# In a bidirectional gated recurrence, the convolution's centre tap is moved ahead of the square roots on ScalarE and its lower part ahead of the scans on VectorE

## The chip, the cores and the metric

The kernel runs on one core of one Trainium2 chip. The metric is the time of one execution in microseconds (us) on the device, as the median of several runs. Engines are named as the profile names them: PE is TensorE's matmul and PEld its weight load, DVE is VectorE, ACT is ScalarE, POOL is GpSimd, SP is SyncE; a q behind a name is the engine's queue.

## The reference, cut to what matters

The whole kernel computes one layer of a diffusion backbone: latent attention and a bidirectional recurrence (RG-LRU) side by side, a gated merge, and a convolutional feed-forward part. The change lies in the recurrence. For each of its 1280 channels it takes the projected input `xb`, runs a centred convolution of width 4 over time, forms two gates per direction from the result, and scans over time, forwards and backwards:

```python
xc = dwconv(xb, lru_conv_w, lru_conv_b, 2, 1)        # four taps, shifts -2, -1, 0, +1
r = sigmoid(xc_blocks @ w_a + b_a)                    # 10 blocks of 128 channels, 2 directions
i = sigmoid(xc_blocks @ w_x + b_x)
log_a = -8 * r * softplus(-lam)
a = exp(log_a)
u = sqrt(-expm1(2 * log_a)) * (i * xc)
h[t] = a[t] * h[t - 1] + u[t]                         # hb: the same from the end
y_b = ((hf + hb) * gelu(yb)) @ w_o_lru
```

Time has 256 context steps and 1024 latent steps, 1280 columns together.

## The kernel before

Products are made in fp32 from two parts: a higher part `hi` (a copy rounded to fp32r, made by ScalarE) and a lower part `lo` (the source minus `hi`, made by VectorE). Each product is three matmuls: hi by hi, hi by lo, lo by hi (`product`, `split`).

The recurrence is `lru`. It works through ten blocks of 128 channels (`for b in range(NB + 1)`; the eleventh round only finishes the last block). TensorE, ScalarE and VectorE run in the order in which the code is written (`manual_schedule`); for GpSimd and SyncE a scheduler sets the order. The recurrence is a pipeline of two blocks: in round `b`, the projections and gates of block `b` are made, and the two scans (`chains`, one for each direction) of block `b - 1`.

What TensorE does in a round: `z(3)` projects `xb` of the block over three column segments into the PSUM tile `z`; `z(2)` projects the gelu branch over two; a merge gate is projected into two tiles `f`; then `gate` is called four times and multiplies the convolution's parts `xh` and `xl` with the gate weights into tiles `g`. `z` and `g` share one PSUM tag with two buffers, so the third `g` needs the buffer from which the first sigmoid (`gate`, L692) reads.

What ScalarE does in a round: a copy `whi` and a copy `ghi` (weights' higher parts), two exponentials (`exp`, L706), two square roots (`root`, L716), the convolution's centre tap with its bias (`xc`, L677), the higher part `xh` (L684), a weight copy, the gelu `gy` (L779), two sigmoids of the merge gate (`gst`, L1218), a weight copy, four gate sigmoids (L692), and two tanh (L703). An ACT_TABLE_LOAD stands where the next function needs another table.

What VectorE does in a round: for each direction three steps between the exponential and the root (`less`, L711, L712, L713); six steps for the other three taps of the convolution (L680 to L682, over the latent and the context columns), which read the product in PSUM and add onto `xc`; for each direction a multiply by the root (L720) and the scans (L723 and L724 forwards, L726 backwards); the lower part `xl` (L771); the gating of the output, weights' lower parts, and three or four steps of the late modulation. These last multiply a weight tile `mw` by a scalar and add onto `macc` (L1238, L1240). GpSimd fetches the `mw` tiles (two buffers), and after every eighth it sums `macc` over the partitions and adds a bias row (L1243, L1246). GpSimd also stores the merge gates (`gld`, from a stage with two buffers) and the recurrence's output (`lrud`).

Of the kernel before, what the change touches and what calls it, by code (L numbers as in the profile page):

```python
# [12 lines left out]
F32 = mybir.dt.float32  # L13
F32R = mybir.dt.float32r
AF = mybir.ActivationFunctionType
OP = mybir.AluOpType
# [7 lines left out]
A = T + C  # L24
# [83 lines left out]
class Block:  # L108
# [494 lines left out]
    def lru(self):  # L603
        tc, nc, a = self.tc, self.nc, self.a
# [27 lines left out]
        with self.pool("lru") as sp, tc.manual_schedule(engines={mybir.EngineType.PE, mybir.EngineType.Activation,  # L632
# [22 lines left out]
            def prepare():  # L655
                if raws:
                    ready.append(self._load_w(None, D, raws.pop(0)))
                    fetch()
# [5 lines left out]
            def z(nseg):  # L664
                ps = pp.tile([P, 3 * 512], F32, tag="z", bufs=2, name=self.name("z"))
                times([(ps[:, c0:c0 + n], self.hrhs(g)) for g, (c0, n) in enumerate(SEGS[:nseg])])
                return ps

            def merge_gate(m):
                st = self.merge_gate(m, *ready.pop(0))  # L670
                prepare()
                nc.gpsimd.dma_start(self.gl_d[m], st)

            def conv(b, ps):
                xc = T5("xc", "xc")
                cw = lambda k: self.vec("cw", 4 * b + k)
                nc.scalar.activation(xc, ps[:, :A], AF.Identity, bias=self.vec("cb", b), scale=cw(2))  # L677
                for c0, n in ((0, T), (T, C)):
                    s, d = ps[:, c0:c0 + n], xc[:, c0:c0 + n]
                    nc.vector.scalar_tensor_tensor(d[:, 2:], s[:, :n - 2], cw(0), d[:, 2:], op0=OP.mult, op1=OP.add)  # L680
                    nc.vector.scalar_tensor_tensor(d[:, 1:], s[:, :n - 1], cw(1), d[:, 1:], op0=OP.mult, op1=OP.add)
                    nc.vector.scalar_tensor_tensor(d[:, :n - 1], s[:, 1:], cw(3), d[:, :n - 1], op0=OP.mult, op1=OP.add)  # L682
                xh, xl = T5("xh", "xh", F32R), T5("xl", "xl", F32R)
                nc.scalar.activation(xh, xc, AF.Copy)  # L684
                return xc, xh, xl

            def gate(b, d, x, w, xh, xl):
                pg = pp.tile([P, 3 * 512], F32, tag="z", bufs=2, name=self.name("g"))
                outs = [(pg[:, c0:c0 + n], lambda k, p, c0=c0, n=n: (xh if p == 0 else xl)[:, c0:c0 + n]) for c0, n in SEGS]
                self.product(outs, lambda k, p: w[p][:, 2 * d + x, :], 1)  # L690
                t = T5(("ta", "tb")[x], "gate", bufs=2)
                nc.scalar.activation(t, pg[:, :A], AF.Sigmoid, bias=self.vec(("ba", "bx")[x], 2 * b + d))  # L692
                return t

            class Chain:
# [19 lines left out]
                def root(c):  # L715
                    nc.scalar.activation(c.s, c.s, AF.Sqrt, scale=-1.0)  # L716

                def scan(c):
                    av, u, s = c.r, c.u, c.s
                    nc.vector.tensor_tensor(u, u, s, op=OP.mult)  # L720
                    cs, ls = slice(T, A), slice(0, T)
                    if c.d == 0:
                        nc.vector.tensor_tensor_scan(s[:, cs], av[:, cs], u[:, cs], 0.0, op0=OP.mult, op1=OP.add)  # L723
                        nc.vector.tensor_tensor_scan(s[:, ls], av[:, ls], u[:, ls], s[:, A - 1:A], op0=OP.mult, op1=OP.add)  # L724
                    else:
                        nc.vector.tensor_tensor_scan(s[:, ::-1], av[:, ::-1], u[:, ::-1], 0.0, op0=OP.mult, op1=OP.add)  # L726

            def gated(gy, hf, hb):
                nc.vector.tensor_tensor(hf[:, :T], hf[:, :T], hb[:, :T], op=OP.add)
                nc.vector.tensor_tensor(gy, gy, hf[:, :T], op=OP.mult)  # L730

            def out(b, gy):
                so = sp.tile([P, 2, T], F32R, tag="lo", bufs=1, name=self.name("lruo"))
                self.split(gy, so[:, 0, :], so[:, 1, :])
                nc.gpsimd.dma_start(self.lru_d[b], so.bitcast(F32))

            def gate_weights(b):
                w = [sp.tile([P, 4, P], F32R, tag=t, bufs=1, name=self.name(t)) for t in ("ghi", "glo")]
                self.split(raws.pop(0)[:, :4 * P], *[t.rearrange("p a b -> p (a b)") for t in w])
                fetch()  # L740
                return w
# [5 lines left out]
            gy, chains = None, []  # L747
            for b in range(NB + 1):
                new = b < NB

                rest = iter(fills[b - 1][1:] if not new else ())
                if new:
                    ps = z(3)
                    prepare()
                    w = gate_weights(b)
                for c in chains:
                    c.exp()
                for c in chains:
                    c.less()
                    if new:  # L760
                        c.root()
                if not new:
                    merge_gate(next(rest))
                    for c in chains:
                        c.root()
                if new:
                    xc, xh, xl = conv(b, ps)
                for c in chains[:1]:
                    c.scan()
                if new:  # L770
                    nc.vector.tensor_tensor(xl, xc, xh.bitcast(F32), op=OP.subtract)  # L771
                for c in chains[1:]:
                    c.scan()
                old = gy
                if new:
                    ps = z(2)
                    prepare()
                    gy = sp.tile([P, T], F32, tag="gy", bufs=2, name=self.name("gy"))
                    nc.scalar.activation(gy, ps[:, :T], AF.Gelu_apprx_tanh)  # L779
                for m in islice(rest, 1):  # L780
                    merge_gate(m)
                if chains:
                    gated(old, chains[0].s, chains[1].s)
                if not new:
                    out(b - 1, old)
                for _ in range(3):
                    next(late, None)
                for m in rest if not new else fills[b][:1]:
                    merge_gate(m)
                if not new:  # L790
                    break
                t = [gate(b, d, x, w, xh, xl) for d in range(2) for x in range(2)]
                if chains:
                    out(b - 1, old)
                chains = [Chain(b, d, t[2 * d], t[2 * d + 1]) for d in range(2)]
                for c in chains:
                    nc.vector.tensor_tensor(c.u, c.u, xc, op=OP.mult)
                    c.tanh()
                next(late, None)
# [1337 lines left out]
```

## Time and profile before

| | |
|---|---|
| median of 3 runs | 1879.92 us (1878.91 to 1880.41) |
| the profiled execution's own time | 1877.24 us |
| its span in the profile | 1875.5 us |
| PE busy | 1829.7 us, 98% |
| PEld busy | 1466.0 us, 78% |
| DVE busy | 1390.0 us, 74% |
| ACT busy | 970.3 us, 52% |
| POOL busy | 383.1 us, 20% |
| mean granted clock of TensorE | 0.994 of full speed |

The span is what the profile sees of one execution; the execution's own time has a little more around it. Busy shares are means over the whole span. The recurrence lies between about 225 and 705 us; times in the trace count from the span's start. A granted clock of 1 is the higher of TensorE's two levels, 2.4 GHz, and one of 0.5 the lower, 1.2 GHz. In a row of the timeline, the text in brackets is how long the engine was idle before the row, and what ended that.

### The profile page before, as it was taken

What the parts mean: (1) busy time and instruction counts of PE and PEld (TensorE: products, weight loads), DVE (VectorE), ACT (ScalarE), POOL (GpSimd) and SP (SyncE); (2) the same over time, 40 slices, a digit from 0 to 9 for tenths busy, and PEclk for the clock granted to TensorE, in tenths of its full rate; (3) what the DMA queues carried; (4) which work ended last, traced back from release to release, by engine and by line L of the source; (5) the groups of instructions that cost most, each with busy time, mean ns of one, the idle gap of its engine ahead of it and who ended that gap; (6) DMA issues with size and microseconds to landing.
All of it is one profiled execution on the core that took longest, in us unless ns stands there. A gap on an engine that the chain in (4) does not pass through costs nothing.

```text
span 1875.5 us, 22292 instructions
## 1 busy us (share of the span) xinstructions
PE 1829.7 (98%) x8180; PEld 1466.0 (78%) x8180; DVE 1390.0 (74%) x1691; ACT 970.3 (52%) x1319; POOL 383.1 (20%) x360
## 2 busy tenths in 40 slices
PE   8999999999999999999999999998999999999998
PEld 3788878887777877888887778876888888888886
DVE  6544668888888858787877775688877777776565
ACT  6434355656565656676666623364444444445452
POOL 0011402020202004676667400000101000010000
PEclk9999999999999999999999999999999999999999
DMA  8125532323332249343432483123443444398671
GB/s 342 57 98 193 216 121 107 129 107 129 118 118 96 95 146 308 109 125 101 125 100 93 135 304 153 64 82 102 185 152 143 155 174 152 140 356 293 214 246 63
DMA packets 109267, 288.29 MB, mean 154 GB/s; under 512 B 14353, under 2 KB 26403, under 8 KB 106854
## 3 DMA queue, kind: packets, MB, share of 16 engines
q1 hardware_dynamic: 85094, 196.04, 30.7%
q0 software_dynamic: 23632, 89.26, 12.4%
q10 hardware_dynamic: 432, 1.57, 0.3%
q8 instruction: 64, 1.05, 0.2%
q14 instruction: 45, 0.37, 0.1%
HBM read 203.30 MB, written 83.52 MB: 153 GB/s over the span
## 4 chain that ended last, share of the span: by engine, by line
PE 61%; issue 24%; DVE 6%; POOL 3%; DMA 3%; ACT 2%; SPq 0%; DVEq 0%; POOLq 0%; ACTq 0%
PE u L1546 18%; PE da L1930 6%; PE f L1038 6%; PE db L1930 4%; PE o L920 4%; PE z L161 2%; PE s L896 2%; PE s L895 2%; PE s L894 2%; PE yo L161 2%; DMA mw<-in_wmod_dram 2%; PE kvps L378 2%; PE x L867 2%; PE f L161 2%; PE ya L161 1%
## 5 line engine op out<-in xcount | busy, mean ns | idle before, releaser
L1546 PE MATMUL u<-b,op 128*128 128x512 f32 x1320 | 312.8, 396 | 7.0 <-ACT pg L1554 2.8
L1546 PEld LDWEIGHTS u<-b,op 128*128 128x128 f32 x1320 | 247.1, 188 | 69.1 <-ACT pg L1554 3.7
L161 PE MATMUL z<-hx,whi 128*128 128x512 f32 x736 | 211.8, 397 | 0.0
L914 POOL TENSOR_TENSOR acc<-acc,p 128x512 f32<-128x512 f32 x120 | 175.8, 1465 | 60.4 <-ACT p L900 56.9
L906 DVE TENSOR_TENSOR pl<-p,ph 128x512 fp32r<-128x512 f32 x160 | 159.9, 1002 | 28.5 <-ACT ph L902 28.1
L161 PE MATMUL f<-hx,whi 128*128 128x512 f32 x480 | 151.0, 396 | 0.0
L900 ACT ACTIVATE p<-s 128x512 f32<-128x512 f32 x160 | 95.6, 597 | 100.0 <-PE s L896 67.7
L161 PEld LDWEIGHTS z<-hx,whi 128*128 128x128 f32 x736 | 126.8, 189 | 25.6
L1915 DVE TENSOR_TENSOR dp<-dr,dp 128x1024 fp32r<-128x1024 f32 x77 | 93.2, 1223 | 56.4 <-PE da L1930 29.9
L1546 PE MATMUL u<-h,op 128*128 128x512 f32 x528 | 127.6, 394 | 0.0
L1546 PEld LDWEIGHTS u<-h,op 128*128 128x128 f32 x528 | 98.4, 188 | 22.8
L161 PE MATMUL z<-hx,wlo 128*128 128x512 f32 x368 | 116.1, 397 | 0.0
L123 DVE TENSOR_TENSOR wlo<-wraw,whi 128x1024 fp32r<-128x1024 f32 (+2 forms) x60 | 67.4, 1125 | 64.1 <-ACT whi L122 64.0
L1038 PE MATMUL f<-l,whi 128*128 128x512 f32 x320 | 108.9, 396 | 0.0
L1930 PE MATMUL da<-dp,dp 128*128 128x512 f32 x352 | 108.4, 389 | 0.0
L161 PEld LDWEIGHTS f<-hx,whi 128*128 128x128 f32 x480 | 90.0, 188 | 21.8 <-ACT r L448 0.2
L1910 ACT ACTIVATE dp<-dr 128x1024 fp32r<-128x1024 f32 x77 | 79.2, 1056 | 52.6 <-PE da L1930 24.8
L868 DVE TENSOR_REDUCE pm<-x 128x1 f32<-128x512 f32 x128 | 83.6, 684 | 29.7 <-PE x L867 20.3
L902 ACT ACTIVATE ph<-p 128x512 fp32r<-128x512 f32 x160 | 101.2, 632 | 5.1
L1512 ACT ACTIVATE op<-wraw 128x512 fp32r<-128x512 f32 x90 | 54.0, 624 | 85.2 <-DVE wraw L1503 62.2
L161 PE MATMUL f<-hx,wlo 128*128 128x512 f32 x240 | 94.9, 395 | 0.0
L1516 DVE TENSOR_TENSOR op<-wraw,op 128x512 fp32r<-128x512 f32 x90 | 61.5, 688 | 33.6 <-ACT op L1512 33.6
(367 smaller groups left out, 3994.4 us busy)
## 6 DMA issues: line engine op xcount, KB each, us to landing
wraw<-in_wz_dram SPq DMA_DIRECT2D x41, 512.0 KB
dr<-da SPq DMA_DIRECT2D x79, 256.0 KB
da<-pg POOLq DMA_DIRECT2D x33, 512.0 KB, 3.7
mw<-in_wmod_dram POOLq DMA_DIRECT2D x32, 512.0 KB, 3.8
wraw<-in_wup_dram SPq DMA_DIRECT2D x23, 512.0 KB
wdr<-in_wdn_dram SPq DMA_DIRECT2D x22, 512.0 KB
db<-wdr POOLq DMA_DIRECT2D x22, 512.0 KB, 2.9
dr<-db SPq DMA_DIRECT2D x44, 256.0 KB
```

The costliest lines, as they stand in the source:

```text
L161: nc.tensor.matmul(ps, wts(k, wp), rhs(k, rp), start=(k == 0 and j == 0), stop=(k == nk - 1 and j == 2))
L868: nc.vector.tensor_reduce(r.pm[:, t, c:c + 1], ps, axis=mybir.AxisListType.X, op=OP.max)
L900: nc.scalar.activation(r.p[b], r.s.pop(b), AF.Exp, scale=SCALE)
L902: nc.scalar.activation(r.ph[b], r.p[b], AF.Copy)
L906: nc.vector.tensor_tensor(r.pl[b], r.p[b], r.ph[b].bitcast(F32), op=OP.subtract)
L914: by.tensor_tensor(r.acc, r.p[0] if b == 1 else r.acc, r.p[b], op=OP.add)
L920: nc.tensor.matmul(r.o, r.v[b // 2][:, b % 2, :], pt.pop(b), start=(b == 0 and n == 0), stop=(b == NT - 1 and n == 1))
L1038: nc.tensor.matmul(f, (hi, lo)[wp][:, k * P:(k + 1) * P], lt[5 * j + k][rp][:, g * 512:(g + 1) * 512], start=(j == 0 and q == 0), stop=(j ...
L1546: self.nc.tensor.matmul(ps, w[wp][:, k * P:(k + 1) * P], self.right(i, k, rp), start=(first and k == 0 and j == 0), stop=(final and k == 3 ...
L1910: self.nc.scalar.activation(self.parts[n][0], self.raws[n], AF.Copy)
L1915: self.nc.vector.tensor_tensor(lo, self.raws.pop(n), hi.bitcast(F32), op=OP.subtract)
L1930: self.nc.tensor.matmul(ps, parts[lp][:, t * P:(t + 1) * P], parts[rp][:, 512:], start=(first and k == 0 and j == 0), stop=(final and k == ...
```

## The change

The function `conv` made the centre tap, the three other taps and the higher part. The centre tap is now a function of its own, `centre`, which is called right after the exponentials. The first multiply of the scan is a step of its own, `drive`. The lower part `xl` stands behind the first chain's `drive` and ahead of its scans.

```diff
-            def conv(b, ps):
+            def centre(b, ps):
                 xc = T5("xc", "xc")
+                nc.scalar.activation(xc, ps[:, :A], AF.Identity, bias=self.vec("cb", b), scale=self.vec("cw", 4 * b + 2))
+                return xc
+
+            def conv(b, ps, xc):
                 cw = lambda k: self.vec("cw", 4 * b + k)
-                nc.scalar.activation(xc, ps[:, :A], AF.Identity, bias=self.vec("cb", b), scale=cw(2))
...
-                return xc, xh, xl
+                return xh, xl
...
+                def drive(c):
+                    nc.vector.tensor_tensor(c.u, c.u, c.s, op=OP.mult)
+
                 def scan(c):
                     av, u, s = c.r, c.u, c.s
-                    nc.vector.tensor_tensor(u, u, s, op=OP.mult)
...
                 for c in chains:
                     c.exp()
+                if new:
+                    xc = centre(b, ps)
                 for c in chains:
                     c.less()
...
                 if new:
-                    xc, xh, xl = conv(b, ps)
+                    xh, xl = conv(b, ps, xc)
+                for c in chains[:1]:
+                    c.drive()
+                if new:
+                    nc.vector.tensor_tensor(xl, xc, xh.bitcast(F32), op=OP.subtract)
                 for c in chains[:1]:
                     c.scan()
-                if new:
-                    nc.vector.tensor_tensor(xl, xc, xh.bitcast(F32), op=OP.subtract)
                 for c in chains[1:]:
+                    c.drive()
                     c.scan()
```

On ScalarE, in the round that makes block 4, the exponentials (`gate`), the table load and the two roots (`s`) stood ahead of the centre tap `xc`. Before:

```order
L706 ACTIVATE gate_2879<-gate_2879,sp_1748 128x1280
L706 ACTIVATE gate_2903<-gate_2903,sp_1748 128x1280
L716 ACT_TABLE_LOAD
L716 ACTIVATE s_2921<-s_2921 128x1280
L716 ACTIVATE s_2922<-s_2922 128x1280
L677 ACTIVATE xc_3025<-z_2930,vecs 128x1280
L684 ACTIVATE xh_3033<-xc_3025 128x1280
```

And of the change, at the same place:

```order
L709 ACTIVATE gate_2879<-gate_2879,sp_1748 128x1280
L709 ACTIVATE gate_2903<-gate_2903,sp_1748 128x1280
L676 ACTIVATE xc_3017<-z_2930,vecs 128x1280
L719 ACT_TABLE_LOAD
L719 ACTIVATE s_2921<-s_2921 128x1280
L719 ACTIVATE s_2922<-s_2922 128x1280
L687 ACTIVATE xh_3033<-xc_3017 128x1280
```

The centre tap went past one table load and two roots; no table load came or went. The same move stands in the rounds of blocks 1 to 9.

On VectorE, at the end of the same round's convolution, the first chain's multiply (`gate`, L720) and its two scans (`s`) stood ahead of the lower part `xl`. Before:

```order
L682 SCALAR_TENSOR_TENSOR xc_3025<-z_2930,vecs,xc_3025 128x255
L720 TENSOR_TENSOR gate_2891<-gate_2891,s_2921 128x1280
L723 SCALAR_TENSOR_TENSOR s_2921<-gate_2879,gate_2891 128x256
L724 SCALAR_TENSOR_TENSOR s_2921<-gate_2879,s_2921,gate_2891 128x1024
L771 TENSOR_TENSOR xl_3034<-xc_3025,xh_3033 128x1280
L720 TENSOR_TENSOR gate_2915<-gate_2915,s_2922 128x1280
L726 SCALAR_TENSOR_TENSOR s_2922<-gate_2903,gate_2915 128x1280
```

And of the change:

```order
L685 SCALAR_TENSOR_TENSOR xc_3017<-z_2930,vecs,xc_3017 128x255
L722 TENSOR_TENSOR gate_2891<-gate_2891,s_2921 128x1280
L778 TENSOR_TENSOR xl_3034<-xc_3017,xh_3033 128x1280
L728 SCALAR_TENSOR_TENSOR s_2921<-gate_2879,gate_2891 128x256
L729 SCALAR_TENSOR_TENSOR s_2921<-gate_2879,s_2921,gate_2891 128x1024
L722 TENSOR_TENSOR gate_2915<-gate_2915,s_2922 128x1280
L731 SCALAR_TENSOR_TENSOR s_2922<-gate_2903,gate_2915 128x1280
```

The lower part went past two scans; the multiply keeps its place. (The scans are named TENSOR_TENSOR_SCAN in the trace.)

On GpSimd, whose order the scheduler sets, the store of a merge gate (`gld`) moved against the fetches of modulation weights (`mw`). Here the queue in the same round, before:

```order
L1247 DMA modd_132<-macc_2498 16x1x64
L1236 DMA mw_1_3110<-in_wmod_dram 128x1024
L672 DMA gld_89<-gst_3116 128x1024
L1236 DMA mw_2_3113<-in_wmod_dram 128x1024
L1236 DMA mw_3_3234<-in_wmod_dram 128x1024
```

And of the change:

```order
L1257 DMA modd_132<-macc_2498 16x1x64
L1246 DMA mw_1_3110<-in_wmod_dram 128x1024
L1246 DMA mw_2_3113<-in_wmod_dram 128x1024
L1246 DMA mw_3_3234<-in_wmod_dram 128x1024
L672 DMA gld_89<-gst_3116 128x1024
```

The store went behind two fetches here; there are seven such places, some with one fetch. The orders of TensorE and SyncE are the same in both programs.

## Rows read from the trace of the kernel before

**Rows 1.** Waits of TensorE, whole span: us in total, times, longest us.

```profile
PE g L161 <- DVE xl L771: 8.2, 3, 3.7
...
PE x L867 <- DMA k<-krd: 0.9, 1, 0.9
```

**Rows 2.** Timeline of TensorE, blocks 3 to 8: start us, us, instruction, idle before.

```profile
379.63 0.74 PE L161 MATMUL g<-xh,ghi 128*128 128x512 f32 x3
...
386.65 0.62 PE L161 MATMUL z<-hx,whi 128*128 128x512 f32 x2
...
400.59 1.10 PE L161 MATMUL z<-hx,whi 128*128 128x512 f32 x4
...
423.00 0.74 PE L161 MATMUL g<-xh,ghi 128*128 128x512 f32 x3
...
433.84 0.62 PE L161 MATMUL z<-hx,whi 128*128 128x512 f32 x2
...
513.55 0.83 PE L161 MATMUL g<-xh,ghi 128*128 128x512 f32 x3
...
527.29 0.62 PE L161 MATMUL z<-hx,whi 128*128 128x512 f32 x2
...
607.00 0.74 PE L161 MATMUL g<-xh,ghi 128*128 128x512 f32 x3
...
616.41 0.62 PE L161 MATMUL z<-hx,whi 128*128 128x512 f32 x2
```

**Rows 3.** Window: length, busy PE PEld DVE ACT POOL, PEclk, DMA share, GB/s.

```profile
517.00:524.00 7.00, 5.94 (x17) 4.88 (x18) 6.96 (x5) 4.81 (x6) 0.54 (x1) 0.51 0.20 78
```

**Rows 4.** Timeline of VectorE, blocks 4, 6 and 8.

```profile
415.43 1.28 DVE L680 SCALAR_TENSOR_TENSOR xc<-z,vecs,xc 128x1022 f32<-128x1022 f32 x1 [2.65 <-ACT xc L677]
...
420.69 1.48 DVE L720 TENSOR_TENSOR gate<-gate,s 128x1280 f32<-128x1280 f32 x1
...
422.20 0.69 DVE L723 TENSOR_TENSOR_SCAN s<-gate,gate 128x256 f32<-128x256 f32 x1
...
425.20 1.47 DVE L771 TENSOR_TENSOR xl<-xc,xh 128x1280 fp32r<-128x1280 f32 x1
...
512.03 1.48 DVE L720 TENSOR_TENSOR gate<-gate,s 128x1280 f32<-128x1280 f32 x1
...
603.25 1.48 DVE L720 TENSOR_TENSOR gate<-gate,s 128x1280 f32<-128x1280 f32 x1
```

**Rows 5.** Line L712: ns min/median/max, first and last start us.

```profile
L712 DVE TENSOR_SCALAR gate<-s x20: 826/828/5042, 266.3 to 672.8; 128x1280 f32<-128x1280 f32 x20
```

**Rows 6.** Waits of VectorE, 303 to 610 us, all of them.

```profile
DVE xc L680 <- ACT xc L677: 18.5, 7, 2.7
DVE macc L1240 <- DMA mw<-in_wmod_dram: 16.5, 6, 2.9
```

**Rows 7.** Timeline of ScalarE, block 4.

```profile
409.02 1.28 ACT L716 ACTIVATE s<-s 128x1280 f32<-128x1280 f32 x1 [10.68 <-DVE s L713]
...
420.87 1.28 ACT L684 ACTIVATE xh<-xc 128x1280 fp32r<-128x1280 f32 x1 [5.47 <-DVE xc L682]
...
428.85 1.33 ACT L692 ACTIVATE gate<-g,vecs 128x1280 f32<-128x1280 f32 x1
```

**Rows 8.** Timeline of GpSimd, blocks 4, 6 and 8.

```profile
417.87 2.40 POOL L1246 TENSOR_TENSOR macc<-macc,bm 1x1024 f32<-1x1024 f32 x1 [8.53 <-issue]
...
509.08 2.41 POOL L1246 TENSOR_TENSOR macc<-macc,bm 1x1024 f32<-1x1024 f32 x1 [8.39 <-issue]
...
598.03 2.39 POOL L1246 TENSOR_TENSOR macc<-macc,bm 1x1024 f32<-1x1024 f32 x1 [6.75 <-issue]
```

**Rows 9.** Timeline, VectorE and GpSimd, at the start of attention.

```profile
715.51 0.68 DVE L906 TENSOR_TENSOR pl<-p,ph 128x512 fp32r<-128x512 f32 x1
...
716.69 1.27 POOL L914 TENSOR_TENSOR acc<-p,p 128x512 f32<-128x512 f32 x1 [21.62 <-ACT p L900]
...
717.30 1.21 DVE L906 TENSOR_TENSOR pl<-p,ph 128x512 fp32r<-128x512 f32 x1 [0.17 <-ACT ph L902]
```

## The prediction

> **What bounds the kernel now.** I read the list of TensorE's waits first. Its longest entry is the one that the change is about: three times the gate products `g` wait for `xl`, the lower part of the convolution, 8.2 us in all [rows 1]. Then I followed the recurrence block by block. The loop at `for b in range(NB + 1)` gives TensorE the same order in each block: `z` over three segments, `z` over two, the merge gate `f`, then `g`. I call the block whose `g` starts at 423.00 block 4; the blocks with a wait are 4, 6 and 8.
>
> TensorE's round, read where it waits for nothing: `g` starts at 379.63 in block 3 and at 423.00 in block 4, so 43.37 us. From there to the next `z` it is 386.65 - 379.63 = 7.02 us without a wait. The same stretch is 10.84 us in block 4 (423.00 to 433.84), 13.74 in block 6 (513.55 to 527.29) and 9.41 in block 8 (607.00 to 616.41) [rows 2]. Over 7.02 these lose 3.82, 6.72 and 2.39: **12.93 us**. That is more than the 8.2 of the list. Part of the rest is the clock: after the longest wait (3.7 us, in block 6) the granted clock was 0.51 from 517 to 524, all but the lower of the two levels, 1.2 GHz [rows 1, 3]. The rest is short waits for ScalarE and the restart.
>
> Why every second block? VectorE's round says so. Its multiply `u0` (L720, first chain) starts at 420.69, 512.03 and 603.25 in blocks 4, 6 and 8: 91.34 and 91.22 us for two rounds, where TensorE needs 2 x 43.37 = 86.74 [rows 2, 4]. So VectorE sets the pace, TensorE catches up with it, and the wait falls in the block where a fast `tensor_scalar` (L712) takes 5.04 us instead of 0.83 [rows 5]. From 303 to 610 us VectorE waits for two things alone: 7 times for ScalarE's centre tap `xc`, 18.5 us (2.65 each), and 6 times for a weight of the late modulation, 16.5 us [rows 6].
>
> **The change, part by part.** *Centre tap ahead of the roots.* ScalarE now makes `xc` right after the two exponentials. VectorE's convolution, which followed the second root (2.65 us idle before it), follows VectorE's own last step at once. Gain: 2.65 us of VectorE per block, so two rounds take 91.34 - 5.30 = 86.04, and 85.92, just under TensorE's 86.74. Cost on ScalarE: it now stands at `xc` until `z` is complete. In block 4 that is at 400.59, where the two-segment products begin [rows 2]; `xc` itself is within the 2.65 that VectorE waited for it. ScalarE idled 10.68 us before the first root at 409.02 [rows 7], and 409.02 - 400.59 - 2.65 = 5.8 are left for the table load, which stands once in either order. A root that came late would first be missed by `u0`, 11.7 us after it (9.0 now). I take nothing.
>
> *Lower part ahead of the scans.* `xl` stood behind the scans of the first chain: 425.20 - 422.20 = 3.00 us [rows 4]. It now follows `u0`. It needs `xh`, which ScalarE starts 0.18 us after `u0` and ends 1.46 after it (1.28 long), while `u0` takes 1.48 [rows 4, 7]: no new wait. The scans move back by `xl`'s 1.47 us; only VectorE's own later steps read them, and the sum of its round is the same. Cost: nothing.
>
> *The queue of GpSimd.* Seven stores of a finished merge gate (`gld`) now stand behind one or two fetches of modulation weights. The store only has to be out before its buffer, one of two, is written again two blocks later, over 80 us; the fetches come no later. Cost: nothing.
>
> *What could come in its place.* GpSimd adds a row to the sum of the modulation (L1246) in blocks 2, 4, 6 and 8; the last three run 417.87 to 420.27, 509.08 to 511.49 and 598.03 to 600.42 [rows 8]. Before, the convolution, which reads one operand in PSUM, lay under it. Moved up by 2.65, `u0` starts at 418.04, 509.38 and 600.60: inside the first two. Does it wait? In attention a two-operand step in SBUF (L906) that began at 717.30, while GpSimd's addition ran from 716.69 to 717.96, took 1.21 us, against 0.68 for the same step alone; from the addition's end it is 0.55 [rows 9]. So I bound the stall of `u0` by nothing and by the rest of the addition: 2.23 us in block 4, 2.11 in block 6, 0 in block 8, and at most the whole 2.40 in block 2. I take the upper values, as that row is nearest.
>
> The Trainium skill (SBUF — State Buffer, "SBUF: two separate sides") speaks against the change here: VectorE and GpSimd share one port pair, an exclusive lock, and a VectorE step with two SBUF inputs is blocked for as long as a GpSimd step that reads SBUF holds it. The row of attention agrees with it; no row of before has `u0` under L1246. By that rule the sum keeps the stalls, without it they fall away, and the two sums differ by the 1.0 us below.
>
> **Do the waits vanish?** VectorE's lead over its old times, counting blocks 2 on: 3 x 2.65 - 2.40 - 2.23 = 3.32 us after `u0` of block 4, 5 x 2.65 - 6.74 = 6.51 in block 6, 7 x 2.65 - 6.74 = 11.81 in block 8. TensorE's lead if all before is recovered: 0, 3.82, 10.54. `xl` ended 5.98 us after `u0` began (425.20 + 1.47 - 420.69) and ends 3.00 sooner beside that.
> - Block 4: 420.69 + 2.98 - 3.32 = 420.35, wanted from 423.00.
> - Block 6: 512.03 + 2.98 - 6.51 = 508.50, wanted from 513.55 - 3.82 = 509.73.
> - Block 8: 603.25 + 2.98 - 11.81 = 594.42, wanted from 607.00 - 10.54 = 596.46.
>
> No wait for `xl` is left. Next late is ScalarE: the third gate product needs the bank that the first sigmoid frees. In block 4 that sigmoid starts at 428.85 and takes 1.33, so it ends 9.49 us after `u0` began [rows 4, 7]; ScalarE's chain starts at the end of the convolution, ahead of the stall. Ends now: 424.63, 512.90, 600.93; wanted half of 7.02 after `g` starts: 426.51, 513.24, 599.97. So 0, 0 and 1.0 us are left; without the stalls none. I take 0.5.
>
> **Sum.** 12.93 - 0.5 = 12.4 us. The profiled execution took 1877.24 (span 1875.5 and 1.74 around it), so 1864.8; it lies 2.7 under the median of the runs shown, 1879.92, from which I subtract the same: **1867.5 us**.
>
> **Rivals.**
> - *VectorE keeps only part of its lead* (it meets a wait for ScalarE or a weight that its lateness hid). With its own block's 2.65 alone, `xl` is in time in block 4 to within 0.3 (426.67 - 3.00 - 2.65 + 2.23 = 423.25), but the sigmoid ends at 427.53, 1.0 late; three such blocks leave 3.1, a gain of 9.8: 1870.1. If the stalls also lift two rounds to 88.2, 1.5 above TensorE's, two pairs lose 2.9 more: 1873.0. For: the waits for weights stay. Against: in 300 us VectorE waited for nothing else [rows 6].
> - *Given back at the recurrence's end.* Attention's first product waits 0.9 us for keys from DRAM [rows 1]; if those came no earlier, that wait would grow by what is won: 1879.9. Against: their loads are issued after the recurrence's last steps and move with them.
> - *Slower.* If `u0` is first at the port, L1246 is pushed behind VectorE's run of two-operand steps, and behind it in GpSimd's queue stand the fetches that VectorE waits for. Two rounds of VectorE must then exceed 91.3, a push of over 5.3 us a pair; at 6.6 in each of three blocks the kernel loses 3.8: 1883.7 or more. Against: L1246 starts 0.17 and 0.30 ahead of `u0`.
> - That the order does not change is excluded: the program's order shows both moves in nine blocks, with no table load added.
>
> **How the numbers follow.** Forecast, all three waits gone: 0.63 (its own range 1865 to 1869.5). Part of the lead: 0.22. Given back: 0.09. Slower: 0.04. More than forecast (timed runs with more half-clock stretches than the profiled one, some 2 us): 0.02. A measurement of this kernel tells 0.2%, 3.8 us, from no change; so faster 0.87, same 0.09, slower 0.04. The range 1864.0 to 1874.0 takes in the first two cases and the last.
>
> **What would show it.** No wait of `g` for `xl`; VectorE's `xc` wait gone; `u0` 3.7 and 3.6 us in blocks 4 and 6; `g` to `z` 7.0 us in every block, 1.0 more at most in block 8; the recurrence 12 us shorter and all later stages as long as now. I am wrong if `u0` meets no addition (then fully 12.9), if waits for the sigmoid appear in each slow block, or if the first key wait grows.

## The result, and the profile after

The changed kernel takes **1862.30 us** in the median of 4 runs (1861.41 to 1864.24), the kernel before 1879.49 us in the same comparison, also 4 runs (1878.91 to 1880.41). The ratio is 0.9913, with a 95% interval of 0.9901 to 0.9925: 17.2 us faster, against 12.4 in the forecast, and 1.7 us below the range's lower end. The profiled execution, one of the four, took 1861.55 us, 15.7 less than that of before, which is not among the four runs of before; its span is 1859.7 us, with a mean granted clock of 0.996.

The waits of TensorE from 225 to 705 us, the recurrence and the start of attention (us in total, times, longest):

```profile
PE s L906 <- ACT q L897: 1.6, 1, 1.6
PE mr L895 <- DVE m L889: 1.3, 1, 1.3
PE g L161 <- ACT gy L789: 0.7, 1, 0.7
PE g L161 <- ACT gate L695: 0.6, 1, 0.6
PE x L877 <- DMA k<-krd: 0.6, 1, 0.6
```

The line of [rows 1] in which `g` waits for `xl` is gone. The first two lines lie in attention and are as long before (1.6 and 1.3 us). What `g` still waits for lies in block 0, where no scan runs yet. The first wait for keys did not grow: 0.6 us, against 0.9 [rows 1].

TensorE's timeline, from the first product of `g` to the next `z` in blocks 4 and 8, and the first `g` of blocks 0 and 9:

```profile
245.07 0.74 PE L161 MATMUL g<-xh,ghi 128*128 128x512 f32 x3
...
420.38 0.74 PE L161 MATMUL g<-xh,ghi 128*128 128x512 f32 x3
...
427.40 0.62 PE L161 MATMUL z<-hx,whi 128*128 128x512 f32 x2
...
593.84 0.74 PE L161 MATMUL g<-xh,ghi 128*128 128x512 f32 x3
...
600.86 0.62 PE L161 MATMUL z<-hx,whi 128*128 128x512 f32 x2
...
637.21 0.74 PE L161 MATMUL g<-xh,ghi 128*128 128x512 f32 x3
```

Both stretches last 7.02 us now, where [rows 2] have 10.84 and 9.41; so do those of the other blocks from 1 on. From block 0 to block 9 it is 637.21 - 245.07 = 392.14 us. I call this length **the recurrence** below. Before, the same two products start here:

```profile
247.71 0.74 PE L161 MATMUL g<-xh,ghi 128*128 128x512 f32 x3
...
652.76 0.74 PE L161 MATMUL g<-xh,ghi 128*128 128x512 f32 x3
```

That is 405.05 us, so 12.91 were won there, the 12.93 of the prediction's losses but for rounding. The rest of the 15.8 us between the two spans: 247.71 - 245.07 = 2.64 lie ahead of the recurrence, where nothing was changed, and some 0.2 behind it.

VectorE's timeline, the first chain's `u0` (L722 now) in blocks 4, 6 and 8, with `xl` (L778) and the first scan (L728) behind the first:

```profile
410.70 3.08 DVE L722 TENSOR_TENSOR gate<-gate,s 128x1280 f32<-128x1280 f32 x1
413.70 1.48 DVE L778 TENSOR_TENSOR xl<-xc,xh 128x1280 fp32r<-128x1280 f32 x1
415.10 0.68 DVE L728 TENSOR_TENSOR_SCAN s<-gate,gate 128x256 f32<-128x256 f32 x1
...
499.06 3.06 DVE L722 TENSOR_TENSOR gate<-gate,s 128x1280 f32<-128x1280 f32 x1
...
586.32 1.48 DVE L722 TENSOR_TENSOR gate<-gate,s 128x1280 f32<-128x1280 f32 x1
```

And GpSimd's addition of a bias row (L1256 now) in the same blocks:

```profile
410.03 2.40 POOL L1256 TENSOR_TENSOR macc<-macc,bm 1x1024 f32<-1x1024 f32 x1 [7.93 <-issue]
...
498.37 2.40 POOL L1256 TENSOR_TENSOR macc<-macc,bm 1x1024 f32<-1x1024 f32 x1 [7.91 <-issue]
...
583.88 2.39 POOL L1256 TENSOR_TENSOR macc<-macc,bm 1x1024 f32<-1x1024 f32 x1 [6.79 <-issue]
```

The new stall is there: `u0` begins inside the addition in blocks 4 and 6, as it does in block 2, and takes 3.08 and 3.06 us instead of 1.48. In block 8 the addition is over by 586.27, `u0` starts behind it and takes its usual time.

ScalarE's timeline in the round of block 4 shows the new order:

```profile
398.17 1.42 ACT L676 ACTIVATE xc<-z,vecs 128x1280 f32<-128x1280 f32 x1 [3.75 <-PE z L161]
399.61 1.28 ACT L719 ACT_TABLE_LOAD   x1
401.77 1.28 ACT L719 ACTIVATE s<-s 128x1280 f32<-128x1280 f32 x1 [0.88 <-DVE s L716]
```

The centre tap waits for `z`, as expected, and the first root still waits 0.88 us for VectorE behind it: here the tap took nothing from the roots. In the rounds of blocks 1, 3 and 9 the first root follows the table load without a wait, so there ScalarE was the later one; but no step of VectorE waits for a root in any round. VectorE's waits from 303 to 610 us, all of them, beside [rows 6]:

```profile
DVE macc L1250 <- DMA mw<-in_wmod_dram: 17.7, 6, 3.9
DVE lruo L123 <- ACT lruo L122: 2.2, 1, 2.2
```

The 18.5 us for `xc` are gone. The waits for weights grew by 1.2 us, all in one of the six (3.9, where [rows 6] have 2.9 at most). I come back to it.

### The profile page after: what moved, and what is told of

Read it like the earlier page. It is cut to its first block, busy times and chain, and to the rows that moved or that the text cites. A ratio compares the mean times of both kernels' runs of the same rounds, so it can differ in the third digit from the quotient of the medians.

```text
span 1859.7 us, 22300 instructions
## 1 busy us (share of the span) xinstructions
PE 1823.2 (98%) x8180; PEld 1462.9 (79%) x8180; DVE 1392.4 (75%) x1691; ACT 972.6 (52%) x1319; POOL 383.5 (21%) x360
## 4 chain that ended last, share of the span: by engine, by line
PE 81%; issue 11%; DVE 4%; ACT 1%; DMA 1%; POOL 1%; SPq 0%; DVEq 0%; POOLq 0%; ACTq 0%
PE u L1556 19%; PE z L161 15%; PE da L1940 6%; PE f L161 6%; PE f L1048 6%; PE db L1940 4%; PE o L930 4%; PE g L161 4%; PE s L906 2%; PE s L905 2%; PE s L904 2%; PE yo L161 2%; PE kvps L378 2%; PE x L877 2%; PE ya L161 2%
```

## The experiments

My theory was the prediction's: the pace of VectorE over two rounds decides. I call it **the pace theory**. Rivals were that the place of `xl` does it (it ends earlier, whatever the pace), and that something outside the recurrence did part of it. A later one was that GpSimd's queue counts.

**The kernel before, again.** No edit.

> The kernel before, a second time, as a control: what do its executions differ in where nothing was changed? Theory 'chance' (the 2.5 us that the changed kernel's profile was ahead when the recurrence began, and the 2.2 us between the first profiled execution and the median of before, are differences between executions and belong to no edit): ratio 1.000 with its interval, spans spread by 1 to 3 us, a longer span going with a lower mean clock, and in this profile the recurrence begins at another time than in the first one, by 0.5 to 3 us; its g-to-z stretches again lose 12.9 us in blocks 4, 6 and 8 together, whichever of them the clock falls in. Theory 'gained elsewhere' (the change wins 2 to 4 us outside the recurrence): this profile begins the recurrence within 0.3 us of the first profile of before.

Measured: 1876.92 us (11 runs) against 1877.75 (23 runs of the kernel before on that chip), ratio 0.9996 [0.9987, 1.0006]. The `g` of block 0 starts at 247.71 again, and the recurrence takes 405.52 us. TensorE waits for `xl` 8.7 us in 3. So the waits belong to the kernel. The shift of the start by chance did not show in this execution; the same start within 0.3 us was the mark of the other theory, and the third executions below decide between them.

**The changed kernel, again.** No edit.

> The whole change a second time, on the chip of the other three. Theory 'chance': 12.9 to 15 us less than before on this chip, ratio 0.992 to 0.993, less than the first time's 17.2. Theory 'gained elsewhere': 17 us again, ratio 0.991, while the profile's recurrence accounts for 13.3 only.

Measured: 1861.56 us (6 runs), ratio 0.9919 [0.9902, 0.9936]. By the medians that is 16.2 us less, between the marks of the two theories. The recurrence takes 392.14 us, as in the first. In block 6 the stall falls on other steps here, as the rows of VectorE and of GpSimd show:

```profile
499.45 1.48 DVE L722 TENSOR_TENSOR gate<-gate,s 128x1280 f32<-128x1280 f32 x1
500.94 3.61 DVE L778 TENSOR_TENSOR xl<-xc,xh 128x1280 fp32r<-128x1280 f32 x1
...
499.59 3.60 POOL L1256 TENSOR_TENSOR macc<-macc,bm 1x1024 f32<-1x1024 f32 x1 [8.74 <-issue]
```

`u0` starts 0.14 us ahead of the addition and keeps its 1.48; the addition takes 3.60 instead of 2.40, and `xl`, which comes next, 3.61 instead of 1.48. This is the first step of the rival "slower" (the addition is pushed behind VectorE), with a push of 1.2 us, where over 5.3 a pair were needed.

**The centre tap alone.** Of the change, `xl` goes back behind the scans:

```diff
-                if new:
-                    nc.vector.tensor_tensor(xl, xc, xh.bitcast(F32), op=OP.subtract)
                 for c in chains[:1]:
                     c.scan()
+                if new:
+                    nc.vector.tensor_tensor(xl, xc, xh.bitcast(F32), op=OP.subtract)
```

> Centre tap ahead of the roots, lower part left behind the scans. Theory 'pace' (VectorE's round of 91.3 us for two blocks sets the pace, and only what shortens the round counts): all of the gain, g to z 7.02 in every block, recurrence 12.9 us shorter, time as the whole change within 1.5 us. Theory 'late product' (xl comes too late in three blocks, and each us by which it comes sooner counts, up to the wait): 2.65 + 2.65 + 1.55 of the waits, so about 7 us, and xl waits of 0.3 and 1.0 left in blocks 4 and 6.

Measured: 1863.61 us (5 runs), ratio 0.9925 [0.991, 0.994]. The recurrence takes 392.15 us, every block from 1 on 7.02 or 7.03, and no `g` waits for `xl`. The centre tap alone gives all of it.

**The lower part alone.** The centre tap goes back behind the roots:

```diff
                     c.exp()
-                if new:
-                    xc = centre(b, ps)
                 for c in chains:
                     c.less()
...
                 if new:
+                    xc = centre(b, ps)
                     xh, xl = conv(b, ps, xc)
```

> Lower part ahead of the scans, centre tap left behind the roots. Theory 'pace': nothing, ratio 1.000 within its interval; the waits for xl shrink to about 1 us, and waits of g for the first sigmoid (the bank of the third gate product) of about 3 us each in blocks 4, 6 and 8 take their place; VectorE's round stays 91.3 us for two blocks. Theory 'late product': 2.98 + 3.00 + 1.55 = 7.5 us less.

Measured: 1876.51 us (11 runs), ratio 0.9998 [0.9987, 1.0009]; the recurrence takes 406.50 us. TensorE's waits:

```profile
PE g L161 <- ACT gate L695: 8.8, 4, 2.7
PE g L161 <- ACT gy L788: 1.4, 3, 0.7
PE x L876 <- DMA k<-krd: 0.9, 1, 0.9
PE g L161 <- DVE xl L777: 0.7, 1, 0.7
```

And VectorE's, 303 to 610 us:

```profile
DVE xc L683 <- ACT xc L676: 18.5, 7, 2.6
DVE macc L1249 <- DMA mw<-in_wmod_dram: 16.6, 6, 2.8
```

An earlier `xl` only hands the same wait to the next that comes late, the buffer that the first sigmoid frees: 8.7 us for `xl` in the control have become 8.8 for the sigmoid. VectorE still waits 18.5 us for the centre tap. The rival of the place falls.

**More work for VectorE.** In the changed kernel, two steps more in each round, into the buffer that `xl` overwrites later, about 2.75 us together. The output does not change.

```diff
+                xh, xl = T5("xh", "xh", F32R), T5("xl", "xl", F32R)
+                if chains:
+                    for n in (A, T):
+                        nc.vector.scalar_tensor_tensor(xl[:, :n], ps[:, :n], 1.0, xc[:, :n], op0=OP.mult, op1=OP.add)
```

> The whole change, and in the rounds of blocks 1 to 9 two more steps of VectorE ahead of its convolution, one operand in PSUM (written into the lower part's buffer, which is overwritten later): about 2.75 us a round, what the centre tap's move took away. Theory 'pace': VectorE's two rounds are back at 91.3 to 91.6 us, the gain is gone although centre tap and lower part keep their new places: time as before within 2 us, waits of g for the first sigmoid of about 3 us in blocks 4, 6 and 8, few for xl. Theory 'order' (the gain lies in where the steps stand, xl before the scans and the convolution ready early): most of the gain stays, 1868 us or less.

Measured: 1876.65 us (10 runs), ratio 0.9999 [0.999, 1.0008]; recurrence 406.86 us. With both moves in place, 2.75 us of VectorE per round take the whole gain away, and the waits are those of the lower part alone (`g` for `gate` 8.8 us in 4, for `xl` 0.7).

**Half as much.** Only the first of the two steps (`for n in (A,)`), 1.48 us.

> The whole change with one of the two extra steps, about 1.45 us a round. Theory 'pace': VectorE's two rounds come to about 89.5 us against TensorE's 86.7, its lead is used up by block 6, some 5 us of waits return, in blocks 6 and 8, so 7 to 8 us less than before, about 1870. If instead each round's excess counted from the first block on: 2.8 us a pair in four pairs, 11 us back, 1875.

Measured: 1875.66 us (10 runs), ratio 0.9995 [0.9984, 1.0006]; recurrence 408.63 us, in a profiled execution that was the slowest of the ten (1880.61). A miss: half the work cost as much as the whole. The second theory's number (1875) came, but not its way: no time is lost up to block 3, and VectorE's two rounds take 92.43 and 92.03 us, not 89.5. The trace shows what else moved. Its GpSimd timeline, behind the `gate` products of block 4:

```profile
434.91 0.53 POOL L1249 DMA_DIRECT2D mw<-in_wmod_dram  x1 [12.86 <-DVE macc L1251]
435.43 0.54 POOL L672 DMA_DIRECT2D gld<-gst  x1
436.23 0.54 POOL L1249 DMA_DIRECT2D mw<-in_wmod_dram  x1 [0.26 <-DVE macc L1253]
```

And VectorE's step that uses the weight:

```profile
441.20 1.28 DVE L1253 SCALAR_TENSOR_TENSOR macc<-mw,cs,macc 128x1024 f32<-128x1024 f32 x1 [5.27 <-DMA mw<-in_wmod_dram]
```

The scheduler, whose order for GpSimd follows from the whole program, had put the merge gate's store between two fetches, in all six of these rounds. VectorE's wait for a weight is 5.27 us here and 24.7 us in its six waits from 303 to 610 us, against 16.5 in [rows 6]. The extra step and the longer waits together undo the gain; their sum follows below.

**No addition on GpSimd.** The changed kernel without L1256; it leaves out the four bias rows of the late modulation.

```diff
-            nc.gpsimd.tensor_tensor(acc[:1], acc[:1], bm, op=OP.add)
```

> The whole change without GpSimd's addition of a bias row (left out: the four bias rows of the late modulation). Theory 'lock' (the multiply u0 is held while that addition reads SBUF): u0 takes 1.47 us in all 20, the 2.8, 3.08 and 3.06 us are gone, and the time does not change against the whole change (within 1 us), since the stall lay within VectorE's lead. If u0's length came from elsewhere (its later place, DMA), the three long ones stay.

Measured: 1862.29 us (4 runs), ratio 0.9923 [0.9908, 0.9939], recurrence 392.14 us. The group of `u0` (ns, min/median/max) in this kernel:

```profile
L722 DVE TENSOR_TENSOR gate<-gate,s x20: 1466/1474/1484, 275.6 to 666.9; 128x1280 f32<-128x1280 f32 x20
```

and in the changed kernel:

```profile
L722 DVE TENSOR_TENSOR gate<-gate,s x20: 1465/1474/3078, 275.0 to 666.3; 128x1280 f32<-128x1280 f32 x20
```

Without the addition `u0` never stalls, so the stall is the addition's doing; and the time is the same, so it costs nothing here.

**The kernel before without GpSimd's work on the sum.** The all-reduce and the addition are left out of the old order, so that the modulation is not summed over the partitions.

```diff
-            nc.gpsimd.partition_all_reduce(acc, acc, P, RED.add)
...
-            nc.gpsimd.tensor_tensor(acc[:1], acc[:1], bm, op=OP.add)
```

> The kernel before without GpSimd's all-reduce and addition in the late modulation (both left out, so the modulation is not summed over the partitions); order of before. Theory 'pace': the step L712 takes 0.83 us in all 20, VectorE's two rounds fall from 91.3 to about 87.1 us, 0.4 above TensorE's 86.7; of the 12.9 us of waits at most 1 to 2 are left; time 11 to 13 us less than before, about 1866. If the waits came from the order of the steps alone and not from the length of the round, the waits for xl stay near 8 us.

Measured: 1862.99 us (4 runs), ratio 0.9921 [0.9904, 0.9939], recurrence 392.14 us, no wait for `xl`; by the medians 13.6 us less, a little over the 11 to 13 expected. VectorE still waits 18.5 us for the centre tap and 16.5 for weights, as in [rows 6]. The fast `tensor_scalar` of [rows 5], which took up to 5042 ns there:

```profile
L712 DVE TENSOR_SCALAR gate<-s x20: 826/827/829, 266.8 to 660.4; 128x1280 f32<-128x1280 f32 x20
```

Taking 4.2 us out of every second round of VectorE, with the old order kept, does the same as moving the centre tap. This is the strongest support of the pace theory: of these two places at which VectorE is relieved, either does.

**Less work than half.** One step over 256 columns (0.42 us), and over 512 (0.68 us), in the changed kernel.

> The changed kernel with one step more on VectorE in each block's round, at the convolution, over 256 columns (by the 1.28 us that 1022 columns with an operand in PSUM take, an estimate of 0.35 to 0.45 us a round). Pace theory: VectorE's lead shrinks by about 0.4 us a round, 1.2 to 2.8 us by blocks 4 to 8, about the margin that the first gate sigmoid had; 0 to 3 us of the 12.9 are lost, 1862 to 1865. Rival (it is the order of GpSimd's queue, a store between two fetches, that cost the half ballast its gain): in the first of these rounds the store stands behind the fetches, as in the changed kernel, in a later one between them; if that decides, VectorE's wait for a weight behind that store is over 3.5 us and a wait of TensorE follows it in that pair of blocks alone, 1864 to 1868.

> The same with one step over 512 columns, an estimate of 0.65 to 0.75 us a round. Pace theory: the lead shrinks by about 2.1, 3.5 and 4.9 us by blocks 4, 6 and 8, over the margins there; about 5 us of the 12.9 are lost, 1866 to 1869, between the time of the changed kernel and that of the kernel before. If any addition at all brings all the waits back (no pace, but a place), 1875 to 1877. If only the store's place counts, the same time as with 256 columns, since GpSimd's order is the same in both.

Measured: 1868.06 us (4 runs), ratio 0.9947 [0.9931, 0.9962], with 256, and 1867.81 (4 runs), 0.9947 [0.9934, 0.9961], with 512; recurrence 397.77 and 396.40 us. The wait of TensorE with 256 columns:

```profile
PE g L161 <- ACT gate L698: 3.9, 3, 2.1
```

So a third of the gain or more goes with 0.42 us a round, and no more of it with 0.68. The number for 256 was a miss (0 to 3 us lost expected, 5.6 measured), that for 512 came out (about 5 expected, 4.3 measured). The columns are not the only thing that changed. In both kernels the store of a merge gate is issued behind two fetches in the rounds of blocks 2, 4 and 6, as in the changed kernel, and between them in those of blocks 3, 5 and 7. The round of block 3 with 512 columns, first GpSimd's rows, then VectorE's step that uses the weight:

```profile
384.04 0.53 POOL L1249 DMA_DIRECT2D mw<-in_wmod_dram  x1 [29.61 <-DVE macc L1253]
384.56 0.54 POOL L672 DMA_DIRECT2D gld<-gst  x1
385.36 0.53 POOL L1249 DMA_DIRECT2D mw<-in_wmod_dram  x1 [0.26 <-DVE macc L1253]
...
388.93 1.28 DVE L1253 SCALAR_TENSOR_TENSOR macc<-mw,cs,macc 128x1024 f32<-128x1024 f32 x1 [3.87 <-DMA mw<-in_wmod_dram]
```

With the store between two fetches, VectorE waits 3.83 to 3.99 us for the second weight with 256 columns, 3.73 to 4.05 with 512, and 3.62 to 5.27 in the kernel with one step more: twelve times of twelve over the 3.5 that were the rival's mark. With the store in another place the waits in the rounds of blocks 2 to 7 are 2.6 to 3.2 us in all runs, but for 3.87, 3.82 and 3.75, all in the round of block 4. (In the rounds of blocks 0 and 1 they are 2.75 to 4.25 in any order.) The second fetch is issued 1.32 us after the first either way (384.04 and 385.36 here, 426.88 and 428.20 in the changed kernel), so it is not the issue that comes later. No run moved the store alone, so that it causes the longer waits is likely, but not shown.

The rival and the pace theory do not exclude each other: a longer wait for a weight is a part of VectorE's round. From `u0` in block 4 to `u0` in block 8, four rounds, the parts add up. Each is the difference to the changed kernel in us:

| kernel | extra columns | waits for weights, blocks 4 to 7 | stalls of `u0`, blocks 4 and 6 | sum | measured |
|---|---|---|---|---|---|
| 256 columns more | +1.7 | +2.3 | -0.6 | +3.3 | +3.5 |
| 512 columns more | +2.7 | +1.1 | -1.5 | +2.3 | +2.6 |
| one step more | +5.9 | +4.8 | -2.1 | +8.6 | +8.8 |
| two steps more | +11.0 | -1.0 | -3.2 | +6.8 | +7.2 |

So 256 columns cost as much as 512, and one step as much as two, since the longer waits and the shorter stalls happened to make up the difference. (The 1.4 us by which the recurrence is longer with 256 are about what the clock takes: it is 0.86 from 600 to 612 us there, behind TensorE's wait, and 1.00 with 512.) What counts is the pace that results: the time from `u0` in block 4 to `u0` in block 8, taken like 586.32 - 410.70 above.

| kernel | `u0`, block 4 to 8, us | recurrence, us | median, us |
|---|---|---|---|
| changed, no addition | 173.59 | 392.14 | 1862.29 |
| before, no GpSimd sum | 174.22 | 392.14 | 1862.99 |
| centre tap alone | 175.28 | 392.15 | 1863.61 |
| changed | 175.62 | 392.14 | 1862.30 |
| 512 columns more | 178.18 | 396.40 | 1867.81 |
| 256 columns more | 179.15 | 397.77 | 1868.06 |
| lower part alone | 182.48 | 406.50 | 1876.51 |
| before | 182.56 | 405.05 | 1879.49 |
| two steps more | 182.85 | 406.86 | 1876.65 |
| one step more | 184.46 | 408.63 | 1875.66 |

TensorE needs 4 x 43.37 = 173.48 us for these four rounds. Up to 175.62 (176.51 in the changed kernel's second execution) the lead that VectorE has when it enters them is enough; beyond, the recurrence grows with the pace. (The last four medians lie within what a measurement tells.) The order of the first two columns is the same but for the closest pair, lower part alone and before. Each row is one execution (the kernel before has 182.97 and 182.78 us, with 405.52 and 406.22, in two others), and the two columns are not independent, since a wait of TensorE also delays the `z` of VectorE's next round. That the pace is the cause is shown by the edits, not by the table.

**Both kernels a third time**, for the 2.64 us ahead of the recurrence.

> The changed kernel a third time, for the part of the difference that lies outside the recurrence. If the half-clock stretch about 87 us after the first product comes and goes by chance, it may be there this time, and the span is then some 2 us longer at the same 392.14 us from the g of block 0 to that of block 9. If the change itself took it away, it is absent again. Time 1861 to 1865, ratio to the kernel before 0.991 to 0.993.

> The kernel before a third time, one look: the same question from the other side. By chance: the stretch about 87 us after the first product may be absent. By the change: it is there, as in the first two. The waits of g for the lower part of the convolution are there again, 8 to 9 us in 3, and the g of block 0 to that of block 9 takes 405 to 406 us.

Measured: the changed kernel 1863.46 us (5 runs), ratio 0.9923 [0.9911, 0.9936]; the kernel before 1878.83 in its one run, `g` waiting for `xl` 9.8 us in 3, recurrence 406.22 us, both a little over what was expected (8 to 9, and 405 to 406). The window from 60 to 100 us (columns as in [rows 3]) of the changed kernel, first execution:

```profile
60.00:100.00 40.00, 40.00 (x216) 32.26 (x216) 20.34 (x24) 15.67 (x19) 0.00 (x0) 1.00 0.19 66
```

and third:

```profile
60.00:100.00 40.00, 40.00 (x204) 31.44 (x203) 20.45 (x27) 13.58 (x14) 0.00 (x0) 0.96 0.19 66
```

In the third the granted clock is 0.96 there, as in all three executions of the kernel before: a short stretch at the lower level, with TensorE busy for the whole 40 us in either. The `g` of block 0 starts at 247.33 in the third, 2.26 us later than in the first, and the recurrence is 392.14 us again. One program shows both, so the change is not needed to explain those 2 us.

## Why the prediction was right in its mechanism and wrong in its number

**What bounds the kernel: right.** VectorE's round sets the pace, and the losses were 12.93 us. Shown by relief at either place (centre tap moved, or GpSimd's sum left out) and by two steps of work added back.

**Centre tap: right.** The `xc` wait is gone, no step waits for a root that came later, and the centre tap alone brings the whole gain. But the 86.04 us for two rounds was the pace without stalls. Measured are 499.06 - 410.70 = 88.36 and 586.32 - 499.06 = 87.26, both above TensorE's 86.74. The kernel runs on the lead of the early blocks. So the rival in which the stalls lift two rounds to 88.2 had the pace right; the loss that it added to it did not come.

**Lower part ahead of the scans: right.** It costs nothing, and gains nothing by itself.

**GpSimd's queue at no cost: right in this kernel, not in general.** With the changed order one wait is 3.87 us instead of some 2.75, which the lead covered. In the kernels with a store between two fetches the waits behind it are 3.6 to 5.3 us, and there they counted. Why the weight comes later there, though its fetch is issued at the same distance, was not separated.

**Stalls of `u0`: right in kind, too high in price.** They are 1.60 and 1.58 us in blocks 4 and 6, not 2.23 and 2.11, since `u0` began 0.67 and 0.69 us into the addition instead of 0.17 and 0.30. In block 4 the addition ends at 412.43 and `u0` at 413.78, 1.35 later, nearly the whole of its 1.48. That is what the Trainium skill says (SBUF — State Buffer, "SBUF: two separate sides"): the one that starts first holds the port pair for its whole instruction. The trace agrees, in block 6 of the second execution the other way round: there `u0` was first, and the addition became longer.

**The 0.5 us left over: wrong, by 0.5.** No block lost anything; the sum for the recurrence is 12.9.

**The step that failed is the last one:** "it lies 2.7 under the median of the runs shown, 1879.92, from which I subtract the same". I took the 2.7 us between the profiled execution and the median of three runs for something that both kernels have. It was not: the changed kernel's profiled execution (1861.55) lies 0.75 under its median (1862.30). Nor does the kernel before keep it. It has medians of 1877.75, 1876.56 and 1877.56 us over 23, 19 and 9 later runs, so that its profiled execution (1877.24) was an ordinary one and the first runs were long ones: only 11 of these 51 later runs reach 1878.91, the shortest of the first. Why those were so long stays open. Without that step the same sum gives 1864.8, 2.5 from the measured time.

**A second term was put at nothing: the time outside the recurrence.** That "all later stages as long as now" held to some 0.2 us, but of the part ahead of the recurrence the prediction says nothing, and there the two profiled executions differ by 2.64. In the third execution 2.26 of them are back, so the change did not win them. The miss of 5.2 us (1867.5 to 1862.30) is then 0.5 for block 8, 2.8 outside the recurrence, 1.5 for the distances to the medians (2.25 before, 0.75 changed), and 0.4 by which the median of before fell from 1879.92 to 1879.49. The range left 3.5 us for more gain than forecast, and the prediction gave such a gain (by half-clock stretches, some 2 us) a chance of 0.02; one such stretch fewer ahead of the recurrence is a part of what came.

**The loss was also read from one execution.** The kernel before takes 405.05, 405.52 and 406.22 us for the recurrence in its three traces, since its waits differ from one execution to the next; the changed kernel takes 392.14 in all of its three. The mean gain there is 405.60 - 392.14 = 13.5 us, and the profile I had was at the low end.

With that, 17.2 us are 13.5 in the recurrence and 3.7 outside it. The other two comparisons give 16.2 and 14.1 us by their medians, and the three ratios of the changed kernel, 0.9913, 0.9919 and 0.9923, stand for 16.4, 15.2 and 14.5 us, so the remainder shrinks to some 1 to 3 us. Its known parts are chance (2 us ahead of the recurrence, which the third execution did not have) and up to 0.6 us at the first keys, 0.9 to 1.2 us before and 0.6 to 1.2 after. Outside the recurrence the three profiled executions of before take 1470.4, 1473.3 and 1470.8 us, those of the changed kernel 1467.6, 1470.8 and 1469.5, in the mean 2.2 less. Of these about 1.1 are the clock's, an estimate from the granted clock around each stretch at the lower level (0.83 from 88 to 98 us is 1.7 us, for example; in all 6.3 us in the mean before, 5.1 changed). Whether the other 1.1 are systematic stays open: the three executions of one kernel differ by up to 3.2.

## What to carry to other kernels

Where an engine with a wait in every second round is late, compare the length of two rounds on each engine first: here an earlier result on the late engine only passed the wait on, while relief of its round, at either of two places, brought the gain. Margins like these are thin: here 0.42 us more per round, with the longer waits for weights that came along, cost a third of it, so every stall that an edit moves is worth its row, and the order of a queue that a scheduler sets is to be read again after every edit. And a forecast should take the loss and the time from several executions, and not carry the distance of one profile from a small median over to the changed kernel.

## What the runs showed of the hardware that was not expected

- A stretch at the lower clock level comes and goes between executions of one program while TensorE is busy throughout: the mean granted clock of 60 to 100 us is 0.96 in 11 of the 14 profiles and 1.00 in three (two of them of the changed kernel, one with two steps more). The `g` of block 0 starts at 245.07 to 245.52 us in these three and at 245.70 to 248.25 in the eleven, about 1.9 later in the mean.
- With a store of 512 KB issued between two fetches of 512 KB on GpSimd's queue, VectorE waited 3.62 to 5.27 us for the second in twelve rounds of twelve, where 2.6 to 3.2 is usual in the same rounds, although that fetch was issued no later. So a half-size addition to VectorE's work, which moved the store there, cost as much as the whole one. That the store is the cause was not tested alone.
- A VectorE step with two operands in SBUF, begun inside an addition on GpSimd that works on one partition alone (1x1024), waits for its end: 3.08 us instead of 1.48. Begun 0.14 us ahead of it, it keeps its 1.48, and the addition takes 3.60 instead of 2.40. The convolution's step with an operand in PSUM had lain inside the same addition before (417.87 to 420.27 us in [rows 8]) at its usual 1.28:

```profile
418.06 1.28 DVE L682 SCALAR_TENSOR_TENSOR xc<-z,vecs,xc 128x1023 f32<-128x1023 f32 x1
```
